# Five raw weight tiles instead of four, three a22 buffers instead of two, and fewer activation buffers, in the seven-product blocks of a feed-forward layer

## The chip, the core and the metric

The kernel runs on one core of a Trainium2 chip. The engines of the core work at the same time, each through its own list of instructions in a fixed order: TensorE (PE) multiplies matrices, VectorE (DVE), ScalarE (ACT) and GpSimd (POOL) work elementwise, and SyncE (SP) and POOL also issue DMAs. The time is the device time of one execution in microseconds (us). The profile comes from one further execution of the same program.

## The reference

Two residual layers over 512 tokens of width 1024 in float32: a recurrent layer (two kinds of recurrence) and a dilated-window attention layer. Each is followed by a feed-forward layer. What matters here is the feed-forward layer:

```python
FFN_HIDDEN = -(-8 * D_MODEL // (3 * 256)) * 256      # 2816, 22 blocks of 128
def swiglu_layer(x, norm_g, w_gate_up, w_down):
    h = rmsnorm(x, norm_g)
    g, u = jnp.split(h @ w_gate_up, 2, axis=-1)
    return x + (jax.nn.silu(g) * u) @ w_down
```

## The kernel before

**Products.** Every weight tile is 128 by 1024. A float32 product is made of three passes over rounded parts: `split` (L91 to L94) has ACT copy the weights to a high part `whi` (L93) and DVE subtract it to get the low part `wlo` (L94); PE then does low by high, high by low and high by high. PE needs both parts of a tile before it starts on that tile, and `wlo` comes last.

**A feed-forward layer** (`ffn`, from L717) makes the 22 hidden blocks in three parts, blocks 0 to 7, 8 to 14 and 15 to 21, and each part is followed by its eight down projections (DVE adds their results to `x` in L840). Blocks 0 to 4 are plain. Blocks 5 to 21 are the seven-product blocks (`seven`, L778): gate and up of one block are computed together by seven half-size products, as in Strassen's scheme, instead of eight. One product is 12 matmuls of 128x128 by 128x256. In steady state PE's order for block m is B11 of m, B22 of m-1, T2 of m, T4 of m-1, T1 of m, T3 of m, B21 of m, and then block m+1. The results pass through small DVE and ACT steps: `s` (ACT), `u2` (L792), `m5` (ACT, L797), `u3` (L799), then L800, L807, L812 and L813, and the block's activation is split into a pair of tiles (`xh`, `xl` or `ah`, `al`, `a`). T3 needs `u2`, since it adds into the PSUM tile that `u2` reads; T4 needs `u3` for the same reason.

**Weights of a seven-product block** (`emit`, kind `a1`, L125 to L139). There are four: a1 is the gate tile as it is, s13 is two halves of the weights with two others added, s24 is a sum of s13 and the gate tile, and a22 is half a tile.

- SP loads the gate tile `raw` (L133), the first halves of `s13` (L132, two DMAs of 256 KB) and `a22` (L134).
- POOL then issues two software DMAs that add further weights into `s13` where it lies (L135 and L136). Each waits for the L132 load of its half.
- DVE adds `raw` to `s13` in two steps (L143 and L144) to get s24. L143 waits for L133 and L135.
- a1, s13, s24 and a22 are each split as above.

**Buffers.** `raw` and `s13` both take tiles of the ring "raw" (L101 to L110): three tiles of the pool `wp`, and one more that the layer lends from its own pool `fp`, four in all. Two tiles go to each block. A tile is free again when the last reader of its old content, a `wlo` split on DVE, is done; until then the L132 or L133 for the new content waits. `a22` has two buffers, and `s`, `u2`, `u3` and `m5` have two each. `HOMES` (L709) says which activation tiles block m uses: five pairs "F" in `fp`, or tiles "S" that other stages have used.

**Order.** `weight` (L155) emits the weights of seven-product blocks four specs ahead; the add of a block thus stands about two blocks ahead of the products that use it. The order on each engine is settled when the program is built: a scheduler takes each instruction at the time at which its own model finds operands and buffers ready. So a change of buffers alone moves instructions, on SP and DVE above all. An engine works strictly in that order: while L143 waits, everything behind it on DVE waits too.

Of the kernel before, what the change touches and what calls it, by code (L numbers as in the profile page):

```python
# [10 lines left out]
F32 = mybir.dt.float32  # L11
# [6 lines left out]
P = 128  # L18
# [7 lines left out]
KF = FF // P  # L26
# [3 lines left out]
NSTD = 5  # L30
# [31 lines left out]
def trunk(ctx: ExitStack, tc: tile.TileContext, a):  # L62
    nc = tc.nc
    mm = nc.tensor.matmul
    V, S, G = nc.vector, nc.scalar, nc.gpsimd
# [17 lines left out]
    NRAW, NSPL, AHEAD = 3, 3, 2  # L83
# [8 lines left out]
    def split(src, hi, lo, eng=V):  # L92
        S.copy(hi, src)  # L93
        eng.tensor_tensor(out=lo, in0=src, in1=hi.bitcast(F32), op=ALU.subtract)  # L94
# [5 lines left out]

    def ring(what, stage):  # L101

        own, more = (NRAW, 1) if what == "raw" else (NSPL, 2)
        names = (("raw", F32),) if what == "raw" else (("whi", F32R), ("wlo", F32R))
        pool, bufs = wp, own
        if stage is not None and stage == lent["stage"]:
            lent[what] += 1
            if lent[what] % (own + more) >= own:
                pool, bufs = lent["pool"], more
        return [pool.tile([P, WMAX], dt, tag=n, bufs=bufs, name=n) for n, dt in names]  # L110
# [3 lines left out]
    def emit(j):  # L114
        src, n, kind, stage = specs[j]
        HW = WMAX // 2
        if kind == "plain":
            raw, = ring("raw", stage)
            hi, lo = ring("split", stage)
            step = n if j else n // 4  # L120
            for c in range(0, n, step):
                nc.sync.dma_start(out=raw[:, c:c + step], in_=src[:, c:c + step])
                split(raw[:, c:c + step], hi[:, c:c + step], lo[:, c:c + step], G if src.tensor.name in on_pool else V)
        elif kind == "a1":

            g, u = src
            fp = lent["pool"]
            raw, = ring("raw", stage)
            s13, = ring("raw", stage)
            a22 = fp.tile([P, HW], F32, tag="a22", name="a22", bufs=2)  # L130
            for z in range(2):
                nc.sync.dma_start(out=s13[:, z * HW:(z + 1) * HW], in_=u[:, :HW])  # L132
            nc.sync.dma_start(out=raw, in_=g)  # L133
            nc.sync.dma_start(out=a22, in_=u[:, HW:])  # L134
            nc.gpsimd.dma_start(out=s13[:, :HW], in_=u[:, HW:], accum_op=ALU.add)  # L135
            nc.gpsimd.dma_start(out=s13[:, HW:], in_=g[:, :HW], accum_op=ALU.add)  # L136
            parts.update(raw=raw, s13=s13, a22=a22)
            hi, lo = ring("split", stage)
            split(raw, hi, lo)  # L139
        elif kind == "s24":  # L140
            raw, s13 = parts["raw"], parts["s13"]
            t = lent["pool"].tile([P, WMAX], F32, tag="s24", name="s24", bufs=1)
            V.tensor_tensor(out=t[:, :HW], in0=s13[:, :HW], in1=raw[:, :HW], op=ALU.add)  # L143
            V.tensor_tensor(out=t[:, HW:], in0=t[:, :HW], in1=raw[:, HW:], op=ALU.add)  # L144
            hi, lo = ring("split", stage)
            split(t, hi, lo)
        elif kind == "s13":
            hi, lo = ring("split", stage)
            split(parts["s13"], hi, lo)
        else:  # L150
            hi, lo = (lent["pool"].tile([P, HW], F32R, tag=f"a22{z}", name=f"a22{z}", bufs=1) for z in "hl")
            split(parts["a22"], hi, lo)
        w_of[j] = (hi, lo)

    def weight(i):  # L155
        while emitted[0] < len(specs) and emitted[0] <= i + (AHEAD if specs[emitted[0]][2] == "plain" else 4):
            emitted[0] += 1
            emit(emitted[0] - 1)
        return w_of.pop(i, None)
# [69 lines left out]
    def slot(i, dtype):  # L229
        return [xp.tile([P, T], dtype, tag=f"x{z}{i}", name=f"x{z}{i}") for z in "hl"]  # L230
# [79 lines left out]
    with ExitStack() as rctx:  # L310
# [125 lines left out]
        for g in range(2):  # L436
# [7 lines left out]
            for c in range(NT):  # L444
                s = slice(c * P, (c + 1) * P)
# [260 lines left out]

    HOMES = [("F", i) for i in range(5)] + [("S", i) for i in (8, 9, 10, 11, 4, 5, 6, 7)] + [("F", i) for i in range(5)] + [("S", i) for i in (8, 9, 10, 11)]  # L709

# [4 lines left out]
    def ffn(norm, idx, after):  # L717
        l, gu, dn = idx
        HT = T // 2
        with ExitStack() as fctx:  # L720
            fp = fctx.enter_context(tc.tile_pool(name="fp", bufs=1))
# [47 lines left out]
            def finish(m, tu):  # L769
                z, i = HOMES[m]  # L770
                hi, lo = slot(i, F32R) if z == "S" else [fp.tile([P, T], F32R, tag=f"a{y}{i}", name=f"a{y}") for y in "hl"]
                split(tu, hi, lo)
                act[m] = (hi, lo)

            def small(tag):
                return fp.tile([P, HT], F32, tag=tag, name=tag, bufs=2)

            def seven(m, last):  # L778

# [2 lines left out]
                r1, r2 = (pa.tile([P, T], F32, tag="pa", name="ps_r")[:, :HT] for _ in range(2))  # L782
                r3 = pm.tile([P, T], F32, tag="pm", name="ps_r3")[:, :HT]
                s, u2, u3, m5 = small("s"), small("u2"), small("u3"), small("m5")
                a1 = weight(gu[m]["a1"])
                product(r1, a1, 0, "B11", True)
# [379 lines left out]
```

## Time and profile before

| what | us |
| --- | --- |
| median of 3 runs | 1334.52 (1334.01 to 1335.09) |
| the profiled execution | 1333.48 |
| its span on the core | 1331.6 |
| PE busy | 1296.0 (97% of the span) |
| DVE busy | 928.1 (70%) |
| ACT busy | 645.6 (48%) |
| POOL busy | 180.0 (14%) |

The span is what the trace covers, and starts at 0 us. The six stretches of seven-product blocks begin at 413.2, 486.98 and 598.31 us in the first feed-forward layer and at 1027.6, 1101.41 and 1215.37 us in the second; here they are called part 0, 1 and 2 of layer 0 and of layer 1. Each row of a timeline names the line, the engine, the tiles written and read without their buffer numbers, and, in brackets, how long the engine stood idle before the instruction and what ended that. A tile `s13` appears as `raw`, since it is of that ring; s24 appears as `s`.

### The profile page before, as it was taken

How to read it: one execution, taken by the hardware profiler on the slowest of the kernel's cores; microseconds unless marked ns; L12 is line 12 of the kernel's file. 1: busy time of each engine (PE TensorE's matmuls, PEld its weight loads, DVE VectorE, ACT ScalarE, POOL GpSimd, SP SyncE). 2: the span in 40 equal slices, each digit the busy share in tenths (PEclk: the TensorE clock that was granted, in tenths of full speed). 3: DMA queues.
4: the chain of work that ended last, by engine and by line, in shares of the span. 5: the costliest groups of instructions: out<-in, count | busy, mean ns of one | idle time of the engine just before them, and what ended most of it. 6: DMA issues, size and time to landing. Idle time of an engine off the chain costs nothing.

```text
span 1331.6 us, 18948 instructions
## 1 busy us (share of the span) xinstructions
PE 1296.0 (97%) x7346; PEld 1113.9 (84%) x7346; DVE 928.1 (70%) x1550; ACT 645.6 (48%) x1012; POOL 180.0 (14%) x178
## 2 busy tenths in 40 slices
PE   7999989999999999999999999999999999999998
PEld 6877767788889889889888877877878989889997
DVE  6886789975688558747764666777789746765772
ACT  6743858443455325424443467546654514433540
POOL 0000000000010111011104453354201011111100
PEclk9999989999999999999999999999999999999999
DMA  7323322532454646564632321221245554565541
GB/s 242 112 80 94 96 74 70 163 111 91 143 131 109 173 109 164 162 143 111 158 96 80 95 79 33 64 79 49 66 132 120 158 127 127 144 162 131 148 128 56
DMA packets 58154, 153.46 MB, mean 115 GB/s; under 512 B 6464, under 2 KB 7232, under 8 KB 57936
## 3 DMA queue, kind: packets, MB, share of 16 engines
q1 hardware_dynamic: 48272, 134.43, 32.7%
q0 software_dynamic: 9792, 17.83, 8.6%
q8 instruction: 57, 0.93, 0.3%
q14 instruction: 33, 0.27, 0.1%
HBM read 150.10 MB, written 2.13 MB: 114 GB/s over the span
## 4 chain that ended last, share of the span: by engine, by line
PE 81%; DVE 8%; ACT 4%; DMA 4%; issue 2%; SPq 0%; POOL 0%; DVEq 0%; ACTq 0%; POOLq 0%
PE ps_pr L163 15%; PE ps_pr L164 15%; PE ps_pr L165 15%; PE ps_r L765 6%; PE ps_r L767 6%; PE ps_r L766 6%; DMA raw<-in_w_gu 4%; PE ps_qkv L905 3%; PE ps_qkv L906 3%; PE ps_qkv L907 3%; DVE wlo L94 3%; PE ps_pT L1017 1%; ACT s L996 1%; PE ps_s L988 1%; PE ps_o L1025 1%
## 5 line engine op out<-in xcount | busy, mean ns | idle before, releaser
L93 ACT CAST whi<-raw 128x1024 fp32r<-128x1024 f32 (+2 forms) x223 | 227.4, 1022 | 327.1 <-PE ps_pr L165 208.8
L163 PE MATMUL ps_pr<-xh,wlo 128*128 128x512 f32 x704 | 279.7, 397 | 13.0 <-DVE wlo L94 12.3
L164 PE MATMUL ps_pr<-xl,whi 128*128 128x512 f32 x704 | 277.7, 394 | 0.6 <-DVE xl L245 0.6
L165 PE MATMUL ps_pr<-xh,whi 128*128 128x512 f32 x704 | 276.6, 393 | 0.0
L94 DVE TENSOR_TENSOR wlo<-raw,whi 128x1024 fp32r<-128x1024 f32 (+2 forms) x191 | 224.4, 1181 | 42.1 <-ACT whi L93 41.2
L163 PEld LDWEIGHTS ps_pr<-xh,wlo 128*128 128x128 f32 x704 | 133.5, 190 | 42.4 <-DVE wlo L94 13.1
L164 PEld LDWEIGHTS ps_pr<-xl,whi 128*128 128x128 f32 x704 | 133.4, 189 | 29.7 <-DVE xl L245 1.8
L165 PEld LDWEIGHTS ps_pr<-xh,whi 128*128 128x128 f32 x704 | 133.3, 189 | 28.6 <-issue 0.6
L840 DVE TENSOR_TENSOR x<-ps_pr,x 128x512 f32<-128x512 f32 x48 | 33.2, 691 | 96.8 <-PE ps_pr L165 96.6
L94 POOL TENSOR_TENSOR wlo<-raw,whi 128x1024 fp32r<-128x1024 f32 x32 | 78.0, 2438 | 167.1 <-ACT whi L93 167.1
L135 POOL DMA_DIRECT2D raw<-in_w_gu x34 | 30.4, 893 | 482.8 <-DMA raw<-in_w_gu 191.8
L765 PE MATMUL ps_r<-xh,wlo 128*128 128x256 f32 x272 | 77.1, 283 | 0.0
L767 PE MATMUL ps_r<-xh,whi 128*128 128x256 f32 x272 | 77.0, 283 | 0.0
L766 PE MATMUL ps_r<-xl,whi 128*128 128x256 f32 x272 | 77.0, 283 | 0.0
L907 PE MATMUL ps_qkv<-whi,xh 128*128 128x512 f32 x192 | 75.5, 393 | 0.0
L905 PE MATMUL ps_qkv<-whi,xl 128*128 128x512 f32 x192 | 75.4, 392 | 0.0
L906 PE MATMUL ps_qkv<-wlo,xh 128*128 128x512 f32 x192 | 75.3, 392 | 0.0
L93 ACT CAST whi<-s 128x1024 fp32r<-128x1024 f32 x34 | 35.8, 1052 | 71.2 <-PE ps_pr L165 37.4
L143 DVE TENSOR_TENSOR s<-raw 128x512 f32<-128x512 f32 x34 | 23.5, 691 | 56.3 <-DMA raw<-in_w_gu 54.5
L163 PE MATMUL ps_pr<-ah,wlo 128*128 128x512 f32 x160 | 62.3, 389 | 0.0
L164 PE MATMUL ps_pr<-al,whi 128*128 128x512 f32 x160 | 62.3, 389 | 0.0
L165 PE MATMUL ps_pr<-ah,whi 128*128 128x512 f32 x160 | 62.2, 389 | 0.0
(372 smaller groups left out, 3074.7 us busy)
## 6 DMA issues: line engine op xcount, KB each, us to landing
raw<-in_w_gu SPq DMA_DIRECT2D x54, 512.0 KB, 3.6
raw<-in_w_in SPq DMA_DIRECT2D x35, 512.0 KB, 3.6
raw<-in_w_gu SPq DMA_DIRECT2D x68, 256.0 KB, 3.4
raw<-in_w_gu POOLq DMA_DIRECT2D x68, 256.0 KB, 5.5
raw<-in_w_dn SPq DMA_DIRECT2D x32, 448.0 KB, 3.9
raw<-in_w_qkv SPq DMA_DIRECT2D x24, 512.0 KB, 3.5
a<-in_w_gu SPq DMA_DIRECT2D x34, 256.0 KB, 3.9
raw<-in_w_out SPq DMA_DIRECT2D x16, 512.0 KB, 3.6
```

What stands on the lines that cost most here:

```text
L93: S.copy(hi, src)
L94: eng.tensor_tensor(out=lo, in0=src, in1=hi.bitcast(F32), op=ALU.subtract)
L163: mm(ps, lhsT=wl[ws], rhs=xh[xs], start=start, stop=False)
L164: mm(ps, lhsT=wh[ws], rhs=xl[xs], start=False, stop=False)
L165: mm(ps, lhsT=wh[ws], rhs=xh[xs], start=False, stop=stop)
L765: mm(ps, lhsT=wl[:, c:c + P], rhs=fh, start=first and k == 0, stop=False, skip_group_check=not first)
L766: mm(ps, lhsT=wh[:, c:c + P], rhs=fl, start=False, stop=False, skip_group_check=not first)
L767: mm(ps, lhsT=wh[:, c:c + P], rhs=fh, start=False, stop=k == 3, skip_group_check=not first)
L840: V.tensor_tensor(out=x[m], in0=ps, in1=x[m], op=ALU.add)
L905: mm(pss[t], lhsT=xl[:, ts_], rhs=wh[:, cols], start=(k == 0), stop=False)
L906: mm(pss[t], lhsT=xh[:, ts_], rhs=wl[:, cols], start=False, stop=False)
L907: mm(pss[t], lhsT=xh[:, ts_], rhs=wh[:, cols], start=False, stop=(k == KD - 1))
```

## The change

The ring "raw" gets two lent tiles instead of one, five in all. `a22` gets three buffers instead of two. Room for this is made in two places: the small tiles `u2`, `u3` and `m5` get one buffer each instead of two (`s` keeps two), and the "F" pairs go from five to four. Block 4's activation moves from the fifth "F" pair to the "S" tile 8, and blocks 15 to 18 and 19 to 21 change places, from "F" to "S" and from "S" to "F".

```diff
-        own, more = (NRAW, 1) if what == "raw" else (NSPL, 2)
+        own, more = (NRAW, 2) if what == "raw" else (NSPL, 2)
...
-            a22 = fp.tile([P, HW], F32, tag="a22", name="a22", bufs=2)
+            a22 = fp.tile([P, HW], F32, tag="a22", name="a22", bufs=3)
...
-    HOMES = [("F", i) for i in range(5)] + [("S", i) for i in (8, 9, 10, 11, 4, 5, 6, 7)] + [("F", i) for i in range(5)] + [("S", i) for i in (8, 9, 10, 11)]
+    NF = NSTD - 1
+    HOMES = [("F", i) for i in range(NF)] + [("S", i) for i in (8, 9, 10, 11, 4, 5, 6, 7)] + [("F", i) for i in range(3)]
+    HOMES += [("S", i) for i in (8, 9, 10, 11)] + [("F", i) for i in range(NF)]
+    assert len(HOMES) >= KF
...
             def small(tag):
-                return fp.tile([P, HT], F32, tag=tag, name=tag, bufs=2)
+                return fp.tile([P, HT], F32, tag=tag, name=tag, bufs=2 if tag == "s" else 1)
```

Line numbers from `HOMES` on are higher by three in the changed kernel (L792 becomes L795, L840 becomes L843). PE's order stays the same product by product. On DVE, L143 moves forward for 20 of its 34 blocks; for six of these it now stands right ahead of a `wlo` split.

First place, on DVE in part 2 of layer 0. `s24_5836` is the sum for block 20, `wlo_5605` the low part of s13 of block 18, `wlo_5671` that of a1 of block 19, and `u2_5658` is block 18's. Before:

```order
L94 TENSOR_TENSOR wlo_5705<-s24_5701,whi_5704 128x1024
L94 TENSOR_TENSOR wlo_5605<-raw_5527,whi_5604 128x1024
L807 TENSOR_TENSOR tg_5517<-ps_r3_5521,u2_5523 128x256
L94 TENSOR_TENSOR wlo_5671<-raw_5661,whi_5670 128x1024
L792 TENSOR_TENSOR u2_5658<-ps_r_5655,s_5657 128x256
L812 TENSOR_TENSOR tu_5518<-ps_r_5520,s_5522 128x256
L813 SCALAR_TENSOR_TENSOR tu_5518<-tu_5518,tg_5517 128x512
L94 TENSOR_TENSOR a22l_5636<-a22_5528,a22h_5635 128x512
L143 TENSOR_TENSOR s24_5836<-raw_5797,raw_5796 128x512
L94 TENSOR_TENSOR al_5736<-tu_5518,ah_5735 128x512
L799 TENSOR_TENSOR u3_5659<-ps_r_5655,s_5657 128x256
```

With the change, at the same place on DVE:

```order
L94 TENSOR_TENSOR wlo_5705<-s24_5701,whi_5704 128x1024
L143 TENSOR_TENSOR s24_5836<-raw_5797,raw_5796 128x512
L94 TENSOR_TENSOR wlo_5605<-raw_5527,whi_5604 128x1024
L144 TENSOR_TENSOR s24_5836<-s24_5836,raw_5796 128x512
L810 TENSOR_TENSOR tg_5517<-ps_r3_5521,u2_5523 128x256
L94 TENSOR_TENSOR wlo_5671<-raw_5661,whi_5670 128x1024
L795 TENSOR_TENSOR u2_5658<-ps_r_5655,s_5657 128x256
```

L143 for block 20 moved forward by seven instructions, past the splits of s13 of block 18 and of a1 of block 19 and past `u2` of block 18.

Second place, on DVE in part 2 of layer 1. `s24_11855` is the sum for block 19, `wlo_11624` the low part of s13 of block 17, `wlo_11690` that of a1 of block 18, and `u2_11677` is block 17's. Before:

```order
L94 TENSOR_TENSOR wlo_11724<-s24_11720,whi_11723 128x1024
L94 TENSOR_TENSOR wlo_11624<-raw_11546,whi_11623 128x1024
L807 TENSOR_TENSOR tg_11536<-ps_r3_11540,u2_11542 128x256
L94 TENSOR_TENSOR wlo_11690<-raw_11680,whi_11689 128x1024
L792 TENSOR_TENSOR u2_11677<-ps_r_11674,s_11676 128x256
L812 TENSOR_TENSOR tu_11537<-ps_r_11539,s_11541 128x256
L813 SCALAR_TENSOR_TENSOR tu_11537<-tu_11537,tg_11536 128x512
L94 TENSOR_TENSOR a22l_11655<-a22_11547,a22h_11654 128x512
L143 TENSOR_TENSOR s24_11855<-raw_11816,raw_11815 128x512
```

With the change, on DVE:

```order
L94 TENSOR_TENSOR wlo_11724<-s24_11720,whi_11723 128x1024
L143 TENSOR_TENSOR s24_11855<-raw_11816,raw_11815 128x512
L94 TENSOR_TENSOR wlo_11624<-raw_11546,whi_11623 128x1024
L144 TENSOR_TENSOR s24_11855<-s24_11855,raw_11815 128x512
L810 TENSOR_TENSOR tg_11536<-ps_r3_11540,u2_11542 128x256
L94 TENSOR_TENSOR wlo_11690<-raw_11680,whi_11689 128x1024
L795 TENSOR_TENSOR u2_11677<-ps_r_11674,s_11676 128x256
```

L143 for block 19 moved forward past the same three kinds of work: the splits of s13 of block 17 and of a1 of block 18, and `u2` of block 17.

Third place, on POOL at the start of layer 1, as a piece of the difference; `nrt` is the norm's reciprocal root, which PE needs to spread it over the tokens (L277, `ps_rb`).

```order
 L94 TENSOR_TENSOR wlo<-raw,whi 128x1024 x2
+L135 DMA raw<-in_w_gu 128x512
+L136 DMA raw<-in_w_gu 128x512
 L271 TENSOR_TENSOR nrt<-rv,mhalf 128x4
 L135 DMA raw<-in_w_gu 128x512
```

The two accumulating DMAs of the first seven-product block, block 5, moved ahead of `nrt`. It is the only move on POOL.

## Rows read from the trace of the kernel before

**Rows 1.** The page: busy time, and the chain that ended last.
```profile
PE 1296.0 (97%) x7346; PEld 1113.9 (84%) x7346; DVE 928.1 (70%) x1550; ACT 645.6 (48%) x1012; POOL 180.0 (14%) x178
...
PE 81%; DVE 8%; ACT 4%; DMA 4%; issue 2%; SPq 0%; POOL 0%; DVEq 0%; ACTq 0%; POOLq 0%
```

**Rows 2.** The windows view of five of the six stretches; the header names the columns.
```profile
core 0: us, PE busy (x) PEld busy (x) DVE busy (x) ACT busy (x) POOL busy (x), PEclk, DMA share, GB/s
413.20:443.44 30.24, 30.24 (x254) 30.23 (x253) 23.54 (x34) 17.00 (x26) 0.00 (x0) 1.00 0.43 126
486.98:560.21 73.23, 71.06 (x590) 70.65 (x589) 55.11 (x85) 37.94 (x61) 7.04 (x8) 1.00 0.58 150
598.31:673.71 75.40, 72.29 (x590) 71.00 (x589) 54.89 (x85) 37.49 (x61) 7.07 (x8) 1.00 0.51 131
...
1101.41:1177.28 75.87, 72.97 (x590) 72.15 (x589) 55.09 (x85) 37.40 (x61) 7.07 (x8) 0.98 0.54 137
1215.37:1289.70 74.33, 71.83 (x590) 70.81 (x589) 55.03 (x85) 38.02 (x61) 7.06 (x8) 1.00 0.58 144
```

**Rows 3.** Waits of PE: line waited for, total us, times, longest us.
```profile
PE ps_r L765 <- DVE wlo L94: 7.5, 4, 2.5
...
PE ps_r L765 <- DVE u L799: 1.7, 2, 1.3
```

**Rows 4.** The line view of L143: what ended its idle time (us, times).
```profile
  DMA raw<-in_w_gu: 54.5, 21
```

**Rows 5.** Timeline of DVE, layer 0 part 2: start, length, instruction, [idle before].
```profile
614.95 0.69 DVE L143 TENSOR_TENSOR s<-raw 128x512 f32<-128x512 f32 x1 [3.06 <-DMA raw<-in_w_gu]
...
620.06 1.22 DVE L94 TENSOR_TENSOR wlo<-raw,whi 128x1024 fp32r<-128x1024 f32 x1
...
630.43 1.22 DVE L94 TENSOR_TENSOR wlo<-raw,whi 128x1024 fp32r<-128x1024 f32 x1
...
640.54 0.69 DVE L143 TENSOR_TENSOR s<-raw 128x512 f32<-128x512 f32 x1 [5.36 <-DMA raw<-in_w_gu]
641.14 0.68 DVE L94 TENSOR_TENSOR al<-tu,ah 128x512 fp32r<-128x512 f32 x1
```

**Rows 6.** Timeline of PE in the same part, the rows with idle time.
```profile
642.22 0.39 PE L765 MATMUL ps_r<-t10h,a22l 128*128 128x256 f32 x1 [1.27 <-DVE u L799]
645.42 0.39 PE L765 MATMUL ps_r<-t00h,wlo 128*128 128x256 f32 x1 [1.50 <-DVE wlo L94]
```

**Rows 7.** Timelines of SP and POOL, issues for blocks 20 and 21 in that part.
```profile
631.67 2.27 SPq L132 DMA_DIRECT2D raw<-in_w_gu  x4
...
634.95 0.88 POOL L135 DMA_DIRECT2D raw<-in_w_gu  x1 [18.91 <-DVE tu L813]
```

**Rows 8.** Timelines of SP and DVE, layer 1 part 2: the chain of its block 19.
```profile
1235.56 3.30 SPq L132 DMA_DIRECT2D raw<-in_w_gu  x4
...
1245.20 0.69 DVE L143 TENSOR_TENSOR s<-raw 128x512 f32<-128x512 f32 x1 [4.77 <-DMA raw<-in_w_gu]
```

**Rows 9.** Line view of L135, 1090 to 1180 us: us from issue to landing.
```profile
DMA to landing us min/median/max: 4.5/5.8/7.0
```

**Rows 10.** Timeline of DVE and PE, layer 1 part 2, around 1226 to 1240 us.
```profile
1226.73 1.23 DVE L94 TENSOR_TENSOR wlo<-raw,whi 128x1024 fp32r<-128x1024 f32 x1 [0.65 <-ACT whi L93]
...
1238.41 0.28 PE L765 MATMUL ps_r<-t00h,wlo 128*128 128x256 f32 x1
...
1239.85 0.28 PE L765 MATMUL ps_r<-t10h,wlo 128*128 128x256 f32 x1
```

**Rows 11.** Timelines of SP, POOL and PE at the start of layer 1.
```profile
973.65 0.33 SPq L133 DMA_DIRECT2D raw<-in_w_gu  x1
...
978.04 1.40 POOL L271 TENSOR_TENSOR nrt<-rv,mhalf 128x4 f32<-128x4 f32 x1 [18.89 <-DVE rv L269]
...
983.19 1.05 PE L277 MATMUL ps_rb<-cst,nrt 128*128 128x128 f32 x8
```

## Prediction, made before the changed kernel was run

> **What bounds the kernel now.** I read the page first: PE is busy for 1296.0 of 1331.6 us and makes 81% of the chain that ended last, DVE 8% and DMAs 4% [rows 1]. PE bounds the kernel, so only what makes PE wait is worth time. The change touches the seven-product blocks, so I read their stretches next [rows 2]. A block has 84 matmuls; part 0 with its three blocks takes 30.24 us for 252 matmuls, 0.12 us each, and nothing is lost. The other parts have seven blocks, 588 matmuls, which at that pace take 70.56 us. They take 73.23, 75.40, 75.87 and 74.33 us: 2.67 + 4.84 + 5.31 + 3.77 = **16.6 us lost**. This is what the change can give back; the rest of PE's idle time lies elsewhere and the change moves nothing there.
>
> What PE waits for in these parts is DVE, a late low part or a late `u` [rows 3]; those named waits are some 10 us. The rest is products stretched by operands that came just late, and slower matmuls: part 1 of layer 1 has a mean granted clock of 0.98 of the full 2.4 GHz, the others 1.00 [rows 2].
>
> DVE has room. In part 2 of layer 0 it is busy for 54.89 us in seven periods of 10.08 us, 7.8 us in each, which leaves 2.2 us [rows 2]. It is late because L143 stands and waits for a DMA: 54.5 us over 21 occasions [rows 4]. One occasion shows the whole case. In part 2 of layer 0, SP issues the L132 loads at 631.67, POOL issues the accumulate L135 at 634.95 [rows 7], and L143 can start only at 640.54 after 5.36 us of idleness [rows 5]. Behind it on DVE stand the split of an activation and `u3` (L799). PE waits 1.27 us for that `u3` at 642.22 and 1.50 us for the next low part at 645.42 [rows 6]. So the chain from a free tile to a finished s13 took 640.54 - 631.67 = 8.9 us here, and in part 2 of layer 1 1245.20 - 1235.56 = 9.6 us [rows 8]. Its short end is some 3.3 us from L132 to L135 [rows 7] plus the shortest landing, 4.5 us [rows 9], so 7.8 us. With four tiles, two to a block, this chain starts too late.
>
> **The change part by part.**
>
> *The fifth tile.* A tile is now reused one step later in the ring, so s13 of a block waits for an older split. The chain itself keeps its length. For block 20 in part 2 of layer 0 the tile's last reader is the split of s13 of block 17, which ended at 620.06 + 1.22 = 621.28 [rows 5]. That was delayed by the 3.06 us that L143 for block 18 stood at 614.95 [rows 5]; without it, it ends at 618.2. The chain then ends at 618.2 + 8.9 = 627.1 instead of 640.5. L143 has moved forward too, so what counts is what stands behind it now: L143, a split, L144, L810, a split, L795, by their lengths 0.69 + 1.22 + 0.68 + 0.42 + 1.22 + 0.42 = 4.65 us, less some 0.09 us at each of five joins where the next begins before the last ends (L143 at 640.54 for 0.69, the next at 641.14) [rows 5], so 4.2 us. `u2` of block 18 is ready at 627.1 + 4.2 = 631.3. T3 of that block lies five products, 7.2 us, before its T4, which without its wait would start at 642.22 - 1.27 = 640.95 [rows 6], so at 633.7, or about 633 once the earlier small losses are gone. Some 1.7 us to spare.
>
> I went through the stalled adds of these parts in this way, with the split that frees each tile and the place of L143 in the new order. In part 1 of both layers and for the other blocks of part 2, the chain ends before L143's turn or within 1 us after it, and DVE's 2.2 us take that up. So nearly all of the 16.6 us goes. For the near misses I take off 0.2 us (bounds 0 and 0.8, the spread of the chain less what is spare).
>
> *A new stall.* One block comes out worse. In part 2 of layer 1, s13 of block 19 gets the tile of a1 of block 17, whose split runs at 1226.73 for 1.23 us, to 1227.96 [rows 10]; it cannot run sooner, as it waits for ACT there. The chain ends at 1227.96 + 7.8 to 9.6 = 1235.8 to 1237.6. L143 for block 19 cannot run before that. Behind it, since it moved forward, is the same sequence, and `u2` of block 17 ends 4.2 us after the chain, at 1240.0 to 1241.8. T3, which needs it, starts at 1239.85 now [rows 10]. PE loses 0.1 to 1.9 us; T1 at 1238.41 needs the first of the splits, about 1.8 us after the chain, and loses less. I take 1.2 us, from the 8.9 us chain.
>
> By rows the landing is most of the chain (4.5 to 7.0 us, median 5.8) [rows 9]. The Trainium skill, "DMA: Bandwidth & Descriptors", section "Anatomy of one DMA — SWDGE (gpsimd) path", fits a software DMA with 2.0 us plus its bytes over 436e3 per us, which for 256 KB gives an estimate of 2.6 us. The trace disagrees: the shortest landing in that stretch was 4.5 us [rows 9]. By the page the new stall would cost PE nothing, and the sum would be 16.4 us.
>
> *a22's third buffer.* It lets L134 go earlier. No wait of PE or DVE in the parts ends on `a22`'s load, so it is worth 0, and the extra traffic ahead of L132 on SP is covered by a DMA share of 0.58 or less [rows 2]. Without that cover it would lengthen the chain (below).
>
> *Fewer buffers for u2, u3, m5, and four "F" pairs.* `u2` and `u3` are written and read on DVE in order, and a block's value is used up before the next is written some 10 us later; `m5`, written by ACT, is read by L800 within its period. The "S" tiles of blocks 4 and 15 to 18 were last read a whole stage before. All of this is 0; if one such wait did appear it would cost at most a DVE step, 0.4 us, per block.
>
> *POOL at the start of layer 1.* L135 and L136 now stand ahead of `nrt`. Their load takes the tile that now goes to the L133 at 973.65 [rows 11]; 3.3 us later, at 976.95, L135 can start. It takes 0.88 us [rows 7], and L136 as much or, by my estimate, at most twice that, so `nrt` starts at 978.7 to 979.6 and, with its 1.40 us, ends at 980.1 to 981.0 instead of 979.44. PE needs it at 983.19 [rows 11]. Cost 0, with 2.2 us of cover; if the load came 3 us late, about 1 us.
>
> **The sum** is 16.6 - 0.2 - 1.2 = 15.2 us. The profiled execution took 1333.48 us, its span 1331.6 and 1.9 around it, and would take 1318.3. It was 1.0 us under the median of 1334.52, and a gain of the same size from that median gives **1319.3 us**.
>
> **The rivals.**
>
> *The chain grows by 3 us.* More tiles in flight put more loads beside the accumulates. Six L143 now stand right ahead of a split that PE needs soon, where 1 to 2 us are spare. Each would cost 3 - 1.5 = 1.5 us, 9 in all: 1319.3 + 9 = 1328. For it speaks that landings spread from 4.5 to 7.0 us [rows 9]; against it, that the bytes stay the same.
>
> *The kernel becomes slower: L143's new places turn against it.* In the old order only cheap steps stood right behind L143; in the new one, six times, two splits and `u2` stand behind it. A chain longer by x us costs 6 (x - 1.5) there; from x = 4.3, so a chain above some 13.5 us, more is lost than the 16.6 us won. At x = 6 the loss is 27 us and the time 1334.5 - 16.6 + 27 = 1345. What could do it is POOL's descriptor work held up by a DVE that no longer stands idle. The rows speak against it: at 634.95, in DVE's idle time, L135 takes 0.88 us on POOL [rows 7], and the whole chain was no longer at 1235.56 [rows 8], where DVE was at work for the first half of it. The Trainium skill, "SBUF — State Buffer", section "Who interferes with whom", has a DVE instruction with two inputs in SBUF, as the splits and L143 are, contend with POOL work that reads SBUF, and infers that descriptor writing is not of that kind. By that, this rival has no mechanism; the trace agrees as far as it goes, with the 0.88 us and the chains above.
>
> *The change does nothing.* If the wait were for the accumulate alone, and not for the tile, earlier tiles would not help: 1334.5. Against it: the L132 at 631.67 [rows 7] follows at once on a split that ended at 630.43 + 1.22 = 631.65 [rows 5], the one that freed its tile.
>
> **How the numbers follow.** Forecast, with chains of 7.8 to 9.6 us: 0.69, 1317 to 1322. Chain longer by some 3 us: 0.17, 1323 to 1330. No effect, or gain and loss near each other: 0.06, 1332 to 1337. Slower: 0.08, near 1345. The measurement can tell about 0.2%, 2.7 us. Faster is 0.69 + 0.17 = 0.86, same 0.06, slower 0.08. The range from 1316 to 1330 holds the first two cases, and leaves out 0.14 and a little of their edges.
>
> **What would show it.** In the profile after, L143's waits for the DMA should fall from 54.5 us to below 10 us, the largest single one being for block 19 in part 2 of layer 1, and the four parts should take 70.6 to 72 us each. PE's waits on `wlo` and `u` at L765 should be near 1 us in all. The L132 to L143 chain should still be 7.8 to 9.6 us where L143 waits for it. If the chain is above 12 us, the second or the first rival holds. If L143 hardly waits and PE still stands for DVE, then my 2.2 us of DVE slack were wrong. If the gain shows in these parts and the total does not, it was lost in the down projections, where I moved nothing.

## The result

The changed kernel takes **1317.18 us** (median of 4 runs, 1317.02 to 1317.63), the kernel before 1334.8 us (median of 4, 1334.01 to 1339.68). The ratio is 0.9861, 95% interval 0.9837 to 0.9885: faster by 1.4%. Forecast were 1319.3 us and a range from 1316 to 1330. The profiled execution took 1317.16 us against 1333.48, 16.3 us less.

The page of the changed kernel, the parts that answer to [rows 1]: busy time, and the chain that ended last.

```profile
PE 1289.7 (98%) x7346; PEld 1111.1 (84%) x7346; DVE 934.1 (71%) x1550; ACT 649.5 (49%) x1012; POOL 179.9 (14%) x178
...
PE 90%; ACT 4%; DVE 3%; DMA 1%; issue 1%; SPq 0%; POOL 0%; DVEq 0%; POOLq 0%
```

DVE's share of the chain fell from 8% to 3% and that of DMAs from 4% to 1%; PE now makes 90% of it. Where the time came from is seen in the windows view of the six stretches of seven-product blocks, which answers to [rows 2]. The columns are the stretch and its length, PE's busy time with its instructions, the granted clock, the DMA share and GB/s.

```profile
413.03:443.26 30.23, 30.23 (x253) 1.00 0.44 125
486.81:557.36 70.55, 70.55 (x589) 1.00 0.59 147
595.47:666.02 70.55, 70.55 (x589) 1.00 0.53 135
1019.89:1050.12 30.23, 30.23 (x253) 1.00 0.44 129
1093.67:1164.22 70.55, 70.55 (x589) 1.00 0.59 148
1202.33:1273.27 70.94, 70.80 (x590) 1.00 0.53 134
```

588 matmuls at 0.12 us are 70.56 us. Three of the four long stretches now take just that, and the fourth 0.39 us more. Before they lost 2.67, 4.84, 5.31 and 3.77 us; of those 16.6 us, 16.2 are back. The clock of part 1 in layer 1, 0.98 before, is 1.00.

PE's waits on DVE inside the products, 7.5 and 1.7 us at the head of [rows 3], are gone from the list of PE's waits altogether; L768 is the old L765. What is left at its head lies elsewhere:

```profile
PE ps_pr L163 <- DVE wlo L94: 12.1, 3, 6.0
PE ps_s L991 <- DVE m L998: 7.1, 14, 0.8
```

L143 still waits for DMAs, as the line view of it shows against 54.5 us and 21 occasions in [rows 4]:

```profile
  DMA raw<-in_w_gu: 21.0, 6
```

Two of the six lie in the seven-product parts, 3.3 us in all. The other four, 17.6 us, lie in the down projections, where five of the 21 lay before, with 11.8 us. L143 moved forward there too, and in three of the four places it now stands right ahead of an L843 (the old L840), as here in the timeline of DVE (start, length, instruction, idle time before it):

```profile
1173.34 0.69 DVE L143 TENSOR_TENSOR s<-raw 128x512 f32<-128x512 f32 x1 [5.22 <-DMA raw<-in_w_gu]
1173.95 0.68 DVE L843 TENSOR_TENSOR x<-ps_pr,x 128x512 f32<-128x512 f32 x1
```

PE has no wait there. That is idle time of an engine that is not the bottleneck.

### The profile page after: what moved, and what is told of

It is laid out like the page before. It is cut to its first block, busy times and chain, and to the rows that moved or that the text cites. A ratio compares the mean times of both kernels' runs of the same rounds, so it can differ in the third digit from the quotient of the medians.

```text
span 1315.2 us, 18991 instructions
## 1 busy us (share of the span) xinstructions
PE 1289.7 (98%) x7346; PEld 1111.1 (84%) x7346; DVE 934.1 (71%) x1550; ACT 649.5 (49%) x1012; POOL 179.9 (14%) x178
## 4 chain that ended last, share of the span: by engine, by line
PE 90%; ACT 4%; DVE 3%; DMA 1%; issue 1%; SPq 0%; POOL 0%; DVEq 0%; POOLq 0%
PE ps_pr L163 15%; PE ps_pr L164 15%; PE ps_pr L165 15%; PE ps_r L768 8%; PE ps_r L770 8%; PE ps_r L769 8%; PE ps_qkv L908 3%; PE ps_qkv L909 3%; PE ps_qkv L910 3%; PE ps_pT L1020 1%; ACT s L999 1%; PE ps_s L991 1%; PE ps_ao L165 1%; PE ps_ao L163 1%; PE ps_ao L164 1%
## 5 line engine op out<-in xcount | busy, mean ns | idle before, releaser
L163 PE MATMUL ps_pr<-xh,wlo 128*128 128x512 f32 x704 | 279.7, 397 | 13.2 <-DVE wlo L94 12.1
L163 PEld LDWEIGHTS ps_pr<-xh,wlo 128*128 128x128 f32 x704 | 133.2, 189 | 42.5 <-DVE wlo L94 12.9
L843 DVE TENSOR_TENSOR x<-ps_pr,x 128x512 f32<-128x512 f32 x48 | 33.1, 690 | 93.1 <-PE ps_pr L165 92.9
L135 POOL DMA_DIRECT2D raw<-in_w_gu x34 | 30.0, 883 | 495.2 <-DMA raw<-in_w_gu 194.3
L768 PE MATMUL ps_r<-xh,wlo 128*128 128x256 f32 x272 | 77.0, 283 | 0.0
L768 PEld LDWEIGHTS ps_r<-xh,wlo 128*128 128x128 f32 x272 | 52.2, 192 | 0.0
```

Source lines behind the costliest of these rows:

```text
L163: mm(ps, lhsT=wl[ws], rhs=xh[xs], start=start, stop=False)
L768: mm(ps, lhsT=wl[:, c:c + P], rhs=fh, start=first and k == 0, stop=False, skip_group_check=not first)
L843: V.tensor_tensor(out=x[m], in0=ps, in1=x[m], op=ALU.add)
```

## The experiments

Ten kernels were run. Theory: PE lost its 16.6 us because L143, waiting on DVE for the accumulating DMA of s13, held up the low parts and `u` behind it; the fifth tile starts that chain a step earlier. The rivals are named with each run. The median of the kernel before, run beside them, was 1335.3 us for the first four, 1336.9 for the next three and 1334.6 for the last three. In what follows "lost" is the length of the stretches beyond 0.12 us for each matmul, in the profiled execution.

### Which part of the change brings the gain

Five tiles, but two a22 buffers, against the changed kernel:

```diff
-            a22 = fp.tile([P, HW], F32, tag="a22", name="a22", bufs=3)
+            a22 = fp.tile([P, HW], F32, tag="a22", name="a22", bufs=2)
```

> The changed kernel with two a22 buffers again; five raw tiles, four F pairs and single u2, u3 and m5 stay. The order on DVE is that of the changed kernel. Theory (the fifth raw tile starts the chain of s13 earlier, and that is the whole gain): 1317 to 1318 us, L143 waits for the DMA 20 to 23 us in all, the four parts lose under 1 us. Rival (a third a22 buffer matters, because L134 stands in SP's queue ahead of L132 and holds it up until a22 is free): L143's waits come back in the parts, above 30 us in all, and the time lies near the middle, 1322 to 1330 us.

Measured: 1318.01 us (1316.96 to 1321.04), ratio to before 0.9879 (0.9854 to 0.9905); L143's waits 22.9 us; lost 0.8 us, all in part 2 of layer 1. The theory's numbers. The fifth tile alone does it, and the third a22 buffer adds nothing that can be measured.

Three a22 buffers, but four tiles, against the changed kernel:

```diff
-        own, more = (NRAW, 2) if what == "raw" else (NSPL, 2)
+        own, more = (NRAW, 1) if what == "raw" else (NSPL, 2)
```

> The changed kernel with four raw tiles again; three a22 buffers, four F pairs and single u2, u3 and m5 stay. Theory: as before the change, 1333 to 1336 us, L143 waits 50 to 58 us. Rival (SP's queue is held up by L134): a part of the gain, 1322 to 1330 us, L143 waits below 40 us.

Measured: 1336.26 us (1331.54 to 1339.02), ratio 1.0001 (0.9985 to 1.0018); L143's waits 55.1 us. No change, so the theory again.

Only the room for it (four F pairs, single `u2`, `u3` and `m5`), with both edits above together:

> Only what makes room: four F pairs, blocks moved among the activation tiles, single u2, u3 and m5; four raw tiles and two a22 buffers as before. Theory: these wait for nothing and cost nothing, 1333 to 1336 us, the same waits as before the change. Rival (single small tiles make DVE or ACT wait, a cost that the fifth tile hides in the changed kernel): slower, up to 0.4 us for each of 34 blocks, 1338 to 1348 us.

Measured: 1335.67 us (1331.6 to 1339.11), ratio 1.0002 (0.9987 to 1.0018); L143's waits 53.1 us. The room costs nothing. Its windows of the four long stretches stand where [rows 2] stood, within 1.7 us each. In this one profiled execution they lose 13.7 us instead of 16.6, and the attention layer takes 3.0 us more (see the section on the hardware), so that the whole is the same:

```profile
487.04:559.88 72.84, 71.04 (x589) 1.00 0.59 150
597.99:674.09 76.10, 71.97 (x589) 1.00 0.50 130
1104.77:1179.04 74.27, 71.70 (x589) 1.00 0.54 139
1217.15:1289.85 72.70, 71.45 (x589) 1.00 0.58 147
```

### Is it L143's chain?

The kernel before with four tiles, without the accumulates:

```diff
-            nc.gpsimd.dma_start(out=s13[:, :HW], in_=u[:, HW:], accum_op=ALU.add)
-            nc.gpsimd.dma_start(out=s13[:, HW:], in_=g[:, :HW], accum_op=ALU.add)
```

> The kernel before with four raw tiles, without the two accumulating DMAs L135 and L136 of each seven-product block, so s13 lacks two of its three terms. The chain from a free tile to L143 is then the L132 load alone, 2.6 to 4.7 us instead of 7.8 to 9.6. Theory (PE lost 16.6 us because that chain is longer than the time that four tiles leave it): L143's waits fall below 8 us, PE's waits on DVE at L765 below 1 us, 1316 to 1319 us. Rival (DVE has too much to do in a period, and L143's wait only shows where that is paid): L143's wait goes, PE still waits for wlo and u, 1326 to 1334 us.

Measured: 1317.61 us (1316.95 to 1317.87), ratio 0.9872 (0.985 to 0.9894). L143's waits 8.8 us, a little over the 8 expected; nothing lost in any stretch, and no wait of PE at L765. With a short chain four tiles are enough. But the run also took away half a million bytes of software DMA for each block and POOL's work on it, so the next one keeps the chain and takes away the other half.

The kernel before, without the accumulate of the second half only:

```diff
-            nc.gpsimd.dma_start(out=s13[:, HW:], in_=g[:, :HW], accum_op=ALU.add)
```

> The kernel before with four raw tiles, without the accumulate L136 of the second half; that of the first half (L135), for which L143 waits, stays. The second half of s13 lacks a term. DVE's order is that of the kernel before, row by row. Theory (what costs is the chain through L135 up to L143): nothing changes for L143, 50 to 56 us of waits, 1333 to 1338 us. Rival for the run without any accumulates (it was quicker because half of the software DMA traffic and of POOL's work was gone, not because L143's chain was short): a good part of that gain comes here too, 1320 to 1328 us.

Measured: 1331.99 us (1329.32 to 1334.23), ratio 0.9981 (0.9968 to 0.9993). L143 still waits, in the line view (its line is L142 there):

```profile
  DMA raw<-in_w_gu: 49.5, 20
```

13.2 us are still lost in the stretches, where the run without both lost nothing. The time lies just under the theory's range and far from the rival's 1320 to 1328. Half of the software DMAs are worth 0.2% (0.07 to 0.32%); the rest goes with L135. This pair of runs cannot tell L135's place in the chain from its traffic. The later add below can: it keeps every DMA, and the loss is gone.

Not every wait of L143 ended on the accumulate. By the landing times in the trace of the kernel before, L143 waited 17 times inside the stretches. Nine of these waits, 30.5 us, ended when its L135 landed. The other eight, 13.8 us, ended when the load of a gate tile (L133) landed, which takes its tile from the same ring; for block 19 in part 2 of layer 0, for one, the accumulate had landed at 618.14 and L143 ran at 624.98, behind a gate tile that landed at 624.85. Each of PE's seven waits on DVE in the stretches comes next behind one of the nine, so the account of the loss stands.

### What a longer chain costs

The changed kernel with L135 issued twice:

```diff
             nc.gpsimd.dma_start(out=s13[:, :HW], in_=u[:, HW:], accum_op=ALU.add)
+            nc.gpsimd.dma_start(out=s13[:, :HW], in_=u[:, HW:], accum_op=ALU.add)
             nc.gpsimd.dma_start(out=s13[:, HW:], in_=g[:, :HW], accum_op=ALU.add)
```

> The changed kernel with the accumulate of the first half (L135) issued twice for each seven-product block, the second after the first has landed, so s13 holds one term twice. PE's order is the same and DVE's nearly so. The chain of 7.8 to 9.6 us grows by one accumulate, x = 4.5 to 6 us. By the price of the prediction's slower rival, 6 (x - 1.5) = 18 to 27 us are lost and the time is 1335 to 1344 us; PE's waits at L768 are on wlo and u in the places where L143 stands right ahead of a split. Rival (five tiles leave more slack than the prediction gave them, and the loss sets in later): under 9 us lost, 1318 to 1326 us.

Measured: 1341.57 us (1338.04 to 1344.99), ratio to before 1.0043 (1.0028 to 1.0059): slower than before the change, and 24.4 us slower than the changed kernel. The total is the one expected; how it is made up is not. First the chain, in the timelines of SP, POOL and DVE in part 2 of layer 0 (one line has been added above, so L135 and L136 are the two accumulates of the first half and L144 is the old L143):

```profile
622.73 0.80 SPq L132 DMA_DIRECT2D raw<-in_w_gu  x2
...
625.86 0.89 POOL L135 DMA_DIRECT2D raw<-in_w_gu  x1 [8.73 <-DVE tu L816]
...
632.10 0.87 POOL L136 DMA_DIRECT2D raw<-in_w_gu  x1 [4.44 <-DMA raw<-in_w_gu]
...
635.83 0.69 DVE L144 TENSOR_TENSOR s<-raw 128x512 f32<-128x512 f32 x1 [6.21 <-DMA raw<-in_w_gu]
636.44 1.22 DVE L94 TENSOR_TENSOR wlo<-raw,whi 128x1024 fp32r<-128x1024 f32 x1
```

The chain is 635.83 - 622.73 = 13.1 us long. A split stands right behind it, and PE waits 3.66 us for that low part at 637.71. These are the rows of PE with the two longest waits, the second in part 2 of layer 1, and then the windows of the four long stretches, of two short ones behind the first wait and of one behind the second:

```profile
637.71 0.39 PE L769 MATMUL ps_r<-t00h,wlo 128*128 128x256 f32 x1 [3.66 <-DVE wlo L94]
...
1249.50 0.50 PE L769 MATMUL ps_r<-t10h,wlo 128*128 128x256 f32 x1 [4.57 <-DVE u L796]
...
487.76:560.32 72.56, 71.34 (x589) 1.00 0.65 157
598.43:679.15 80.72, 73.68 (x589) 0.98 0.57 138
1109.74:1182.19 72.45, 71.07 (x589) 1.00 0.65 158
1220.30:1297.18 76.88, 72.31 (x589) 0.98 0.59 137
...
637.00:640.00 3.00, 2.21 (x12) 0.77 0.41 104
640.00:644.00 4.00, 3.89 (x25) 0.74 0.66 234
1250.00:1254.00 4.00, 4.00 (x25) 0.62 0.92 237
```

20.4 us are lost, but not evenly at six places as the formula 6 (x - 1.5) had it: 2.0, 10.2, 1.9 and 6.3 us, most of it around two long waits, 3.66 us and 4.57 us. The granted clock falls behind both: to a mean of 0.77 and 0.74 in the first two short windows, 7 us long, where PE so loses some 1.7 us more, and to 0.62 in the third, some 1.5 us. A further 2.9 us go in the attention layer (below). So the formula met the total by luck: the cost sits mostly at two places and not at six, and part of it is a slower clock, for which the formula has no term.

The same, with the add emitted later, as in the next section:

> The changed kernel (five raw tiles) with L135 issued twice for each block as before, so s13 holds one term twice, and with the add of s24 emitted two specs later, which puts L143 behind u3 and two splits, half a block further back on DVE. Theory (what a long chain costs depends on where L143 stands on DVE): the later place gives some 4 to 5 us back to each chain, so most of the 24 us lost with the long chain go, 1317 to 1324 us. Rival (the longer chain as such is too slow for five tiles, whatever DVE's order): 1332 us or more.

Measured: 1317.67 us (1315.96 to 1318.44), ratio 0.9875 (0.9861 to 0.989). The two accumulates are there as in the run before, L143 still waits 35.8 us in all, and PE waits once, for 0.9 us. 24 us went away with the order on DVE alone. That edit does more than give L143 a later place: it also lets tiles come free earlier, as the next section shows, and the loads of block 20 in part 2 of layer 0 go out 12.9 us into the stretch instead of 24.3. But block 19 in part 2 of layer 1 shows the later place by itself. This is its add (L146 here), in a stretch that begins at 1204.22:

```profile
1234.85 0.69 DVE L146 TENSOR_TENSOR s<-raw 128x512 f32<-128x512 f32 x1 [0.77 <-DMA raw<-in_w_gu]
```

It runs 30.6 us into the stretch, when its chain has ended, and that is later than the 27.0 us of the run before. But its turn came only at 29.9 us and not at 20.8, behind the `u2` for which PE had waited 4.57 us, and PE does not wait there.

### Place or tile?

The kernel before, four tiles, nothing left out. The two adds of s24 and its split are emitted with the split of a22, two specs later:

```diff
         elif kind == "s24":
+            return
+        elif kind == "a22":
             raw, s13 = parts["raw"], parts["s13"]
...
             split(t, hi, lo)
+            w_of[j - 2] = (hi, lo)
+            hi, lo = (lent["pool"].tile([P, HW], F32R, tag=f"a22{z}", name=f"a22{z}", bufs=1) for z in "hl")
+            split(parts["a22"], hi, lo)
...
-        else:
-            hi, lo = (lent["pool"].tile([P, HW], F32R, tag=f"a22{z}", name=f"a22{z}", bufs=1) for z in "hl")
-            split(parts["a22"], hi, lo)
```

> The kernel before with four raw tiles, and the add of s24 (L143 and L144) emitted together with the split of a22, two specs later; on DVE it moves back by about half a block, behind u3 and two splits. Nothing is left out. Theory (PE loses because L143 comes up on DVE before its chain has ended; a later place does as well as an earlier chain): L143's waits below 15 us, 1317 to 1323 us. Rival (four tiles are too few as such: with a later add the tiles come free later, and the next chain starts later again): L143's waits stay above 30 us, 1327 to 1336 us.

Measured: 1317.53 us (1317.19 to 1318.32), ratio 0.9861 (0.9837 to 0.9884), the same as the changed kernel's. L143's waits are 12.0 us, all in the down projections, and its windows of the four long stretches (with PE, weight loads, DVE, ACT and POOL) are clean, as these two are:

```profile
596.93:667.48 70.55, 70.55 (x589) 70.55 (x588) 57.39 (x85) 38.52 (x61) 7.11 (x8) 1.00 0.58 143
1203.80:1274.35 70.55, 70.55 (x589) 70.55 (x588) 57.40 (x84) 38.40 (x61) 7.09 (x8) 1.00 0.57 142
```

Four tiles were not too few as such, and the whole gain is to be had without a byte more of SBUF. But the edit does two things at once. It gives L143 a later place, and it puts the split of s13, which frees a tile, ahead of the split of s24. These are the timelines of DVE and SP in part 2 of layer 0: the split of s13 of block 18, which frees the tile of block 20, the L132 of block 20, and its add (L145 here).

```profile
618.41 1.23 DVE L94 TENSOR_TENSOR wlo<-raw,whi 128x1024 fp32r<-128x1024 f32 x1
...
619.66 0.80 SPq L132 DMA_DIRECT2D raw<-in_w_gu  x2
...
636.91 0.69 DVE L145 TENSOR_TENSOR s<-raw 128x512 f32<-128x512 f32 x1
```

Counted from the start of the stretch, the tile comes free at 22.7 us, where it came free at 33.3 before. The accumulate lands at 30.9 us (issued at 623.85, 3.9 us to landing) instead of 42.2; with the fifth tile it was 29.6. L143's turn comes at 40.0 us instead of 36.9. So for this block the chain ends 11 us earlier and L143 comes up 3 us later, and the earlier chain is the greater part: the old end of the chain, 42.2 us, would still lie behind the new turn. What the later place alone would give on four tiles was not tried.

Both together, the changed kernel with the later add:

> The changed kernel with the add of s24 emitted two specs later, nothing left out or doubled. Theory: the last 0.4 us that PE loses in part 2 of layer 1 go, the six stretches take 0.12 us for each matmul, 1316.5 to 1317.5 us, which cannot be told from the changed kernel. Rival (a later add brings s24 too late for T2): PE waits for wlo at T2 in some blocks, 1320 us or more.

Measured: 1317.43 us (1317.05 to 1317.92), ratio 0.9876 (0.9861 to 0.989). Nothing is lost in any of the six stretches, and the time cannot be told from the changed kernel's. This is the floor for what L143 can give; no version was found that beats the changed kernel by more than the measurement tells.

### Six tiles

```diff
-        own, more = (NRAW, 2) if what == "raw" else (NSPL, 2)
+        own, more = (NRAW, 3) if what == "raw" else (NSPL, 2)
...
-            a22 = fp.tile([P, HW], F32, tag="a22", name="a22", bufs=3)
+            a22 = fp.tile([P, HW], F32, tag="a22", name="a22", bufs=2)
...
-                return fp.tile([P, HT], F32, tag=tag, name=tag, bufs=2 if tag == "s" else 1)
+                return fp.tile([P, HT], F32, tag=tag, name=tag, bufs=1)
```

> Six raw tiles instead of five; the room comes from two a22 buffers and one s buffer. Theory: what PE still loses to L143 in part 2 of layer 1 (0.4 us) goes and nothing else is to be had, 1316 to 1318 us, the four parts at 70.6 us each. Rival (a single s buffer makes ACT's copy of r1 wait for L812 of the block before): 0.5 to 1 us in each of 34 blocks, 1330 us or more.

Measured: 1323.84 us (1319.65 to 1324.3), ratio to before 0.9908 (0.988 to 0.9937): better than before, worse than five tiles, and between the two expectations. Two rows of its windows, in the columns of the last view:

```profile
486.96:558.15 71.19, 71.19 (x590) 70.90 (x588) 55.78 (x84) 37.69 (x62) 5.31 (x6) 1.00 0.55 143
1204.40:1275.61 71.21, 71.21 (x590) 70.85 (x588) 55.71 (x84) 37.77 (x62) 5.31 (x6) 1.00 0.49 130
```

Each long stretch takes 0.64 us more than 588 matmuls need, 0.09 for each block, with no wait long enough to be listed. The 0.4 us of part 2 in layer 1 went, as they should, and 3.0 us came in over all six. The timelines of DVE, ACT and PE in part 2 of layer 1 show how:

```profile
1238.00 0.42 DVE L815 TENSOR_TENSOR tu<-ps_r,s 128x256 f32<-128x256 f32 x1
...
1238.79 0.37 ACT L790 COPY s<-ps_r 128x256 f32<-128x256 f32 x1 [0.19 <-ACT a22h L93]
...
1239.05 0.28 PE L770 MATMUL ps_r<-t03h,whi 128*128 128x256 f32 x1
1239.21 0.39 PE L768 MATMUL ps_r<-xh,wlo 128*128 128x256 f32 x1
1239.43 0.28 PE L769 MATMUL ps_r<-xl,whi 128*128 128x256 f32 x1
```

With one `s` buffer, ACT's copy of a block's first result into `s` comes only behind L815 (the old L812), which reads the old content for the block before. B21 adds into the PSUM tile that the copy reads, and its first matmul, at 1239.21, starts just as the copy ends. It and the next start 0.16 and 0.22 us after the one ahead, not 0.12. PE's order is no longer the same either: the first matmuls of B21 now stand ahead of T3. So the rival's mechanism is there, at a tenth to a fifth of its price. The single `s` buffer was not tried alone. The profiled execution is the quickest of the four; the other three took some 4 us more, at a mean granted clock of 0.995 instead of 0.997, and why stays open.

## Why the prediction was right

**The bound and the prize** were right. 16.6 us were counted as lost in the four parts, and 16.2 of them came back.

**The chain** was right. For block 20 in part 2 of layer 0, L132 was forecast at 618.2 and went out at 615.77, with the stretch itself starting 2.8 us earlier; L143 ran at 625.17 after a wait of 1.23 us, and PE lost nothing:

```profile
615.77 0.80 SPq L132 DMA_DIRECT2D raw<-in_w_gu  x2
...
625.17 0.69 DVE L143 TENSOR_TENSOR s<-raw 128x512 f32<-128x512 f32 x1 [1.23 <-DMA raw<-in_w_gu]
```

The near misses, put at 0.2 us, cost 0.

**The new stall** was right in its place and its mechanism, and too large. These are the timelines of SP, DVE and PE in part 2 of layer 1 after the change, where [rows 10] stood:

```profile
1214.94 0.80 SPq L132 DMA_DIRECT2D raw<-in_w_gu  x2
...
1222.81 0.69 DVE L143 TENSOR_TENSOR s<-raw 128x512 f32<-128x512 f32 x1 [2.09 <-DMA raw<-in_w_gu]
1223.42 1.22 DVE L94 TENSOR_TENSOR wlo<-raw,whi 128x1024 fp32r<-128x1024 f32 x1
...
1226.62 0.42 DVE L795 TENSOR_TENSOR u<-ps_r,s 128x256 f32<-128x256 f32 x1
...
1227.10 0.39 PE L768 MATMUL ps_r<-t10h,wlo 128*128 128x256 f32 x1
```

The chain of block 19 is 1222.81 - 1214.94 = 7.9 us, close to the short end of 7.8 and not the 8.9 that was taken. From L143 to the end of `u2` (L795) it is 1227.04 - 1222.81 = 4.2 us, as worked out, and T3 starts at once upon it. PE loses 0.39 us, not 1.2. This term was mis-sized by 0.8 us: the landing was taken from one long chain, where the row with the spread of landings gave the lower end as well.

**POOL, a22 and the smaller buffers** cost nothing, as forecast. `nrt` ended at 973.07 and PE had no wait for it; the runs with the room alone and with a22 alone are the measurements.

**What did not hold.** L143's waits were to fall below 10 us and are 21.0. The longest was to be that of block 19; it is one of 5.22 us in a down projection. The prediction took the 54.5 us as if all of it lay in the stretches, and wrote that it moved nothing in the down projections. L143 did move there, and its waits grew from 11.8 to 17.6 us; they cost PE nothing. All of the 54.5 us was also put down to the accumulate, though some of the waits ended on a gate tile, as told above. The rival with a chain longer by 3 us did not come: from the issue of L132 to the landing of L135 the 34 blocks took 6.9 to 11.5 us before and 7.0 to 11.8 after, with a median of 8.5 and 8.6. That is wider than the 7.8 to 9.6 that the prediction allowed. The price of the slower rival, tested by doubling the accumulate, gave the right total from the wrong parts, by luck, as told above.

**What the prediction did not see** is that the tile is only one of two ways. It wrote that with four tiles the chain starts too late. That holds for the order that DVE had. In the order of the later add the same four tiles came free 10.6 us earlier for block 20, and L143 came up later besides. The changed kernel moved L143 forward, and so spent some of what the fifth tile won.

**The sum.** 15.2 us were forecast; the profiled executions differ by 16.3, which is 15.2 + 0.8 for the stall + 0.2 for the near misses, and 0.1. The medians differ by 17.6 us. The 1.3 us more are in the spread of the kernel before, which is the next section's matter.

## What the runs showed of the hardware

The kernel before is not only slower but wider: 1331.68 to 1339.56 us in the 19 runs beside the first four experiments, with a mean granted clock between 0.993 and 0.998, where the changed kernel's four runs lie within 0.6 us, all at 0.997 (five tiles with two a22 buffers have one run of 1321.04 us, at 0.996). Part of what a late low part costs can come after the wait. In the kernel before, in part 1 of layer 1, PE stands 2.45 us for a low part and resumes at 1148.18. The windows view there (length, PE's busy time, granted clock, DMA share, GB/s) shows the clock at half its full speed, 1.2 instead of 2.4 GHz, from 1149.5 to 1152.6:

```profile
1148.00:1149.00 1.00, 0.82 (x7) 1.00 0.00 0
1149.00:1150.00 1.00, 1.00 (x9) 0.74 0.96 152
1150.00:1151.00 1.00, 1.00 (x5) 0.50 0.85 327
...
1152.00:1153.00 1.00, 1.00 (x7) 0.55 0.81 271
1153.00:1154.00 1.00, 1.00 (x11) 1.00 0.82 264
```

A matmul then starts every 0.21 us instead of every 0.12. The spell costs some 1.5 of the 5.31 us that this part lost. Behind shorter waits in the same execution, 2.06 us at 542.47 and 1.50 us at 645.42, no such spell came. In the runs with four tiles and three a22 buffers, with the room alone, and with the doubled accumulate, another spell lies in the attention layer, around 830 us, which the change does not touch. This is the window there, with three a22 buffers and four tiles:

```profile
830.00:840.00 10.00, 10.00 (x45) 0.68 0.01 2
```

In these three profiles 356.8 to 356.9 us lie between the end of layer 0's last stretch and the start of layer 1's first; in those of the kernel before and of the changed one, which have no spell there, it is 353.9. What decides whether it comes was not tried.

The Trainium skill, "DMA: Bandwidth & Descriptors", section "Anatomy of one DMA — SWDGE (gpsimd) path", fits a software DMA with 2.0 us plus its bytes over 436e3 per us, which gives an estimate of 2.6 us for 256 KB. The trace disagrees: the accumulating ones of this kernel landed 5.4 us after their issue in the changed kernel (median of 68) and 5.5 us in the kernel before, where DVE stood idle behind them for longer. They add into SBUF and run beside other loads; no run here has one alone.

## What to carry to other kernels

When an instruction that waits for a DMA stands in the middle of an engine's fixed order, its wait is paid by everything behind it. Read from the timeline what frees the buffer, when the chain ends, when the instruction comes up, and what stands right behind it. Then there are two cures, an earlier start and a later place. An earlier start comes from another buffer, or from an order in which the last reader of the old content runs sooner. A new order costs no memory and gave as much here, so it is worth trying first; then read again which of the two it changed, since here it changed both. Price a PE wait with what follows it, too: waits of 2.45, 3.66 and 4.57 us were here followed by a slower clock that cost another 1.5 to 1.7 us.
